# Expert stage of a two-layer model: weight splits traced a block earlier, gates and gathers respread, own buffers for the second half's first group

## The chip, the cores and the metric

The kernel runs on one core of a Trainium2 chip. The metric is the device time of one execution in microseconds; the median of three runs is given. The profile is of one further execution.

## The reference

The program is one large layer (a state-space branch, a dilated attention branch, a memory branch, and then a mixture of 16,384 tiny experts, "PEER") followed by two further layers (attention and a 32-expert mixture). All is float32, 512 tokens, model width 1024. The change lies in the PEER stage alone, which computes this:

```python
def _peer(hn, w_query, sub_keys, expert_down, expert_up):
    q = (hn @ w_query).reshape(b, s, PEER_HEADS, 2, PEER_QUERY_DIM // 2)      # 8 heads
    sc = einsum('bshcd,hckd->bshck', q, sub_keys)                             # 2 x 128 keys a head
    v1, i1 = top_k(sc[..., 0, :], 16);  v2, i2 = top_k(sc[..., 1, :], 16)
    cand = v1[..., :, None] + v2[..., None, :]                                # 256 a head
    top, pos = top_k(cand, 16)
    idx = i1 * 128 + i2 at pos;  gate = softmax(top)                          # 128 experts a token
    act = gelu(einsum('bld,blhkd->blhk', hb, expert_down[idx]))
    return einsum('blhk,blhkd->bld', gate * act, expert_up[idx])
```

## The kernel before

**Two ways to compute the experts.** The first 128 tokens (GAT) are done by gathering: for each of their 128 chosen experts a row of 1024 numbers is fetched for every token (an indirect DMA of 512 KB, issued by GpSimd, line 1045) and VectorE (DVE) reduces it against the token (line 1049, rows of expert_down) or adds it, weighted, to a sum (line 1058, rows of expert_up). That makes 2 x 128 steps, called rows here; the generator `gathered` gives one at each call, with five rows in buffers ahead. The other 384 tokens (DENSE) are done densely: all 16,384 experts are computed for them, and a matrix of gates that is zero but for the chosen ones weights the result.

**First half, `peer_down`, lines 1067 to 1135.** After the queries (16 products, lines 1090 to 1105) the dense part runs over 128 blocks of 128 experts. Each block loads a weight of 128x1024 (512 KB) into one of five `raw` buffers on SyncE's queue and splits it, by `wload` (line 250), into a rounded high part on ScalarE (ACT, line 267) and a low remainder on DVE (line 268). Each part has three buffers. TensorE (PE) then does 24 matmuls of 128x384 in three passes (lines 272 to 274) into one of four accumulators `acc`; ACT takes the gelu (line 1124) into one of two buffers `act`, and its own queue stores it to the DRAM tensor `actd` (line 1125).

**Routing beside it.** While the blocks run, DVE also works out the choice. `peer_select` is called for four chunks of 128 tokens (the first is for the gathered tokens; it sets `ready`, after which rows may run). `peer_gates` then builds the gate matrix of the three dense chunks: for each token two one-hot columns (`oa`, half of them on ACT, and `ob`, lines 1281 to 1288), one product of both on PE (line 1289), in 96 pieces of four tokens; a group of 32 tokens is stored to the DRAM tensor `gd` from GpSimd's queue (line 1292).

**What sets the order.** The blocks are a generator that gives way four times a block. Each such turn adds PACE to a credit, and the routing is advanced as long as credit is left; each of its steps names its cost in a `yield` (2.0, 0.8, 5.0, 2.3 in `peer_select`, 2.2 in `peer_gates`, while a selection that runs between the gates costs nothing). A second count, `due`, adds 0.27 a turn for the rows while routing lasts, and 0.5 after it. That is the order in which the instructions are listed. A planner in the kernel's framework (line 2113) then lays them out on the engines by its own timing: of what is ready on an engine, the earliest in the list goes first, so that the final order can differ from the list. On the chip each engine works through its own instructions in that final order.

**Second half, `peer_up`, lines 1137 to 1189.** Sixteen groups of eight blocks. For each group `weighted` loads the stored gelus and gates (`at`, `gt`, four blocks at a time, 768 KB each), multiplies them (every second one on GpSimd, POOL, line 1162) and splits the product into `c_hi` and `c_lo`: eight pieces a group. The pieces of the next group are listed between the eight tiles j of the present one. Each tile loads and splits a weight of expert_up, does 24 matmuls, adds the result to the residual `x` on DVE (line 1178), and advances the rows by 1.1. All of its buffers are in a pool "pu" opened after the first half's pools are closed, so the first group's loads, too, wait until those are free:

Of the kernel before, what the change touches and what calls it, by code (L numbers as in the profile page):

```python
# [24 lines left out]
KC = 8  # L25
# [12 lines left out]
RAW = 20  # L38
PACE = 0.68
GAT = 128  # L40
# [179 lines left out]
class Kernel:  # L220
# [55 lines left out]
    def proj_fm_g(self, src, act, kn=KC, engine=None):  # L276

        hi, lo = self.wload(src, kn * 128, engine)
        act = [[a[:, k] for k in range(kn)] if not isinstance(a, list) else a for a in act]
        n = act[0][0].shape[1]  # L280
        ps = self.ps("acc", [128, 512])
        for k in range(kn):
            sl = slice(k * 128, (k + 1) * 128)
            self.mm3(ps[:, :n], (hi[:, sl], lo[:, sl]), (act[0][k], act[1][k]), k == 0, k == kn - 1)
            if k == kn - 1:
                with self.tc.issue_after(self.last.ins):
                    next(self.side, None)
            if k % 2 == 1:
                yield
        return ps[:, :n]  # L290
# [731 lines left out]
    def peer(self):  # L1022

        TG = 32
        actd = self.dr.tile([128, 128, DENSE], F32, name="actd")
        gd = self.dr.tile([DENSE // TG, 128, 128 * TG], F32, name="gd")
        with self.pool("rows") as pr:
# [3 lines left out]
            self.peer_down(actd, gd, TG, st, rows)  # L1031
            self.peer_up(actd, gd, TG, rows)

# [32 lines left out]

    def peer_down(self, actd, gd, TG, st, rows):

        V, A, P, T, Q, I = self.V, self.A, self.P, self.T, self.Q, self.I
        with self.pool("u2") as up:  # L1070
            hn = [up.tile([128, KC, S], F32R, name=n) for n in ("hn_hi", "hn_lo")]
            acts = [up.tile([128, DENSE], F32, name=f"act{i}") for i in range(2)]
            st["hn"] = st["pool"].tile([128, D], F32, name="rhn", tag="rhn")
# [9 lines left out]
            with self.pool("pk", 1) as p1:  # L1083
                idxu = p1.tile([128, NT, 16, 16], U32, name="idxu")
                vals = p1.tile([128, NT, 16, 16], F32, name="vals")
                with self.pool("pk3", 2) as p2:
# [3 lines left out]
                    for hc in range(16):  # L1090
# [8 lines left out]
                        for c in range(NT):  # L1099
# [5 lines left out]
                            V.max_index(ix[:, 8:16], v[:, 8:16], sc[:, c])  # L1105

                with self.pool("pk2", 2) as p2:
                    def routing():
                        yield from self.peer_select(0, vals, idxu, p2, st)
                        sT = yield from self.peer_select(1, vals, idxu, p2)  # L1110
                        for c in range(1, NT):
                            nxt = _Work(self.peer_select(c + 1, vals, idxu, p2) if c + 1 < NT else iter(()))
                            for i, w in enumerate(self.peer_gates(c, sT, p2, gd, TG)):
                                yield w
                                if i % 4 == 0:
                                    yield next(nxt, 0.0)
# [4 lines left out]
                    def hidden():  # L1121
                        for i1 in range(128):
                            ps = yield from self.proj_fm_g(I["down"][i1], dense)
                            A.activation(acts[i1 % 2], ps, AF.Gelu)  # L1124
                            A.dma_start(actd[i1], acts[i1 % 2])
                    for i, _ in enumerate(hidden()):
                        credit += PACE
                        while credit > 0:
                            credit -= next(work, 1.0e9)
                        if st["ready"]:  # L1130
                            due += 0.27 if credit > -1e8 else 0.5
                            while due >= 1:
                                next(rows, None)
                                due -= 1
                    _run(work)

    def peer_up(self, actd, gd, TG, rows):
        V, A, P, T, Q, I = self.V, self.A, self.P, self.T, self.Q, self.I
        with self.pool("pu", 2) as p2:

            pair = lambda i: [p2.tile([128, 8, DENSE], F32R, name=f"c{i}_{n}", bufs=1) for n in ("hi", "lo")]
            odd = pair(1)
# [4 lines left out]
            def weighted(g):  # L1147

                hi, lo = parts[g % 2]
                for h in range(2):  # L1150
                    i0 = g * 8 + h * 4
                    at = p2.tile([128, 4, DENSE], F32, name="at")
                    queue = P if g == 0 else Q
                    queue.dma_start(at, actd[i0:i0 + 4].rearrange("i p t -> p i t"))
                    gt = p2.tile([128, DENSE // TG, 4, TG], F32, name="gt")
                    queue.dma_start(gt.rearrange("p j i t -> p j (i t)"),
                                gd.rearrange("j p x -> p j x")[:, :, i0 * TG:(i0 + 4) * TG])
                    for i in range(4):
                        k = h * 4 + i
                        a = at[:, i].rearrange("p (j t) -> p j t", t=TG)  # L1160
                        eng = P if i % 2 else V
                        eng.tensor_mul(a, a, gt[:, :, i])
                        self.split(hi[:, k], lo[:, k], at[:, i])
                        yield
                return hi, lo

            nxt, due = weighted(0), 0.0
            for g in range(16):
                hi, lo = _run(nxt)
                nxt = weighted(g + 1) if g < 15 else iter(())  # L1170
                for j in range(KC):
# [19 lines left out]
    def peer_select(self, c, vals, idxu, p2, st=None):  # L1191
# [17 lines left out]
        V.tensor_add(cand[:, :, starts[8]:], vv[:, :, 0, 8:16], vv[:, :, 1, 0:1].to_broadcast([128, 8, 8]))  # L1209
        yield 2.0  # L1210
        top = p2.tile([128, 8, 16], F32, name="top")
        posu = p2.tile([128, 8, 16], U32, name="posu")
        for h in range(8):
# [4 lines left out]
            V.max_index(posu[:, h, 8:16], top[:, h, 8:16], cand[:, h])  # L1218
            yield 0.8

# [21 lines left out]
        yield 5.0  # L1242
        sel = p2.tile([128, 3, 128], F32, name="sel")
        gate = gate.rearrange("p h k -> p (h k)")
        A.activation(sel[:, 2] if st is None else st["gate"], gate, AF.Copy)
        for n, ix in ((0, ia), (1, ib)):
            for z in range(2):
# [7 lines left out]
                V.tensor_reduce(sel[:, n, part], oh, axis=AX.X, op=ALU.add)  # L1255
            yield 2.3
        if st is not None:
# [11 lines left out]
    def peer_gates(self, c, sT, p2, gd, TG):  # L1269
# [3 lines left out]
        for j in range(128 // TG):  # L1273
            st = p2.tile([128, 128, TG], F32, name="gst")
            for t4 in range(TG // 4):
# [14 lines left out]
                A.activation(st[:, :, t4 * 4:t4 * 4 + 4], ps.rearrange("p t i -> p i t"), AF.Copy)  # L1290
                yield 2.2
            P.dma_start(gd[(c * 128 - GAT) // TG + j], st.rearrange("p i t -> p (i t)"))
# [825 lines left out]
```

## Time and profile before

| | us |
|---|---|
| median of three runs (lowest, highest) | 4564.19 (4563.07, 4568.98) |
| the profiled execution | 4570.65 |
| its span in the trace | 4568.8 |

The span's mean granted clock is 0.969 of full speed. Over the whole span PE is busy 4298.5 us (94%), DVE 2732.7 us (60%), ACT 1457.4 us (32%) and POOL 1227.5 us (27%). These shares are averages over many stages. The stage of the change lies at about 940 to 2206 us of the span: the first half up to about 1630, the second half after it. A busy share says nothing by itself; the stretches have to be compared one by one, and the waits named. In the wait and timeline views a number in brackets is the time for which the engine stood idle just before that instruction, with the instruction that released it. Durations on one engine overlap by some tens of nanoseconds, so that a sum of them is larger than the time in which the engine is busy.

### The profile page before, as it was taken

How to read it: one execution, taken by the hardware profiler on the slowest of the kernel's cores; microseconds unless marked ns; L12 is line 12 of the kernel's file. 1: busy time of each engine (PE TensorE's matmuls, PEld its weight loads, DVE VectorE, ACT ScalarE, POOL GpSimd, SP SyncE). 2: the span in 40 equal slices, each digit the busy share in tenths (PEclk: the TensorE clock that was granted, in tenths of full speed). 3: DMA queues.
4: the chain of work that ended last, by engine and by line, in shares of the span. 5: the costliest groups of instructions: out<-in, count | busy, mean ns of one | idle time of the engine just before them, and what ended most of it. 6: DMA issues, size and time to landing. Idle time of an engine off the chain costs nothing. (4 is left out here: it accounts for less than half of the span.)

```text
span 4568.8 us, 59963 instructions
## 1 busy us (share of the span) xinstructions
PE 4298.5 (94%) x21607; PEld 3271.1 (72%) x21607; DVE 2732.7 (60%) x5348; ACT 1457.4 (32%) x2579; POOL 1227.5 (27%) x883
## 2 busy tenths in 40 slices
PE   8998989998999869999999998999989999899997
PEld 7777777898999869999877774544448778545443
DVE  6577776799999789766458764222234665522122
ACT  5324443343677223333334331100122433200001
POOL 2153335017534554210113451000010345100000
PEclk9999999999999989999999998999999999899999
DMA  4133433348999999765334447988852122598986
GB/s 151 55 98 108 129 115 111 112 141 279 347 363 344 365 360 351 265 227 176 109 109 125 136 128 262 371 321 323 341 219 86 57 63 94 223 359 318 350 310 242
DMA packets 351617, 987.41 MB, mean 216 GB/s; under 512 B 34288, under 2 KB 114672, under 8 KB 349392
## 3 DMA queue, kind: packets, MB, share of 16 engines
q1 hardware_dynamic: 293488, 795.77, 49.0%
q0 software_dynamic: 39392, 162.55, 9.8%
q10 hardware_dynamic: 18432, 25.17, 1.5%
q8 instruction: 174, 2.85, 0.2%
q14 instruction: 131, 1.07, 0.1%
HBM read 926.70 MB, written 56.66 MB: 215 GB/s over the span
## 5 line engine op out<-in xcount | busy, mean ns | idle before, releaser
L267 ACT ACTIVATE whi<-raw 128x1024 fp32r<-128x1024 f32 (+3 forms) x582 | 568.2, 979 | 1196.7 <-PE acc L273 701.5
L268 DVE TENSOR_TENSOR wlo<-raw,whi 128x1024 fp32r<-128x1024 f32 (+4 forms) x438 | 536.3, 1227 | 247.6 <-ACT whi L267 227.8
L1752 PE MATMUL acc<-raw,xg 128*64 128x512 f32 (+1 forms) x2024 | 554.7, 599 | 0.0
L272 PE MATMUL acc<-hn_hi,whi 128*128 128x384 f32 (+1 forms) x1152 | 402.7, 350 | 26.8 <-ACT act L1124 26.5
L274 PE MATMUL acc<-hn_hi,wlo 128*128 128x384 f32 (+1 forms) x1152 | 401.0, 349 | 21.5 <-DVE wlo L268 21.5
L273 PE MATMUL acc<-hn_lo,whi 128*128 128x384 f32 (+1 forms) x1152 | 400.1, 347 | 0.0
L349 POOL TENSOR_TENSOR ssq<-ssq,sq 128x512 f32<-128x512 f32 (+1 forms) x22 | 31.4, 1440 | 1338.9 <-ACT sq L348 1338.8
L268 POOL TENSOR_TENSOR wlo<-raw,whi 128x1024 fp32r<-128x1024 f32 (+3 forms) x144 | 281.7, 1958 | 376.2 <-ACT whi L267 369.4
L272 PE MATMUL acc<-c_hi,whi 128*128 128x384 f32 x1024 | 342.7, 336 | 30.9 <-ACT c_hi L267 30.7
L1752 PEld LDWEIGHTS acc<-raw,xg 128*64 128x64 f32 (+1 forms) x2024 | 164.0, 140 | 283.6 <-issue 261.0
L274 PE MATMUL acc<-c_hi,wlo 128*128 128x384 f32 x1024 | 342.8, 336 | 5.1 <-DVE wlo L268 5.0
L273 PE MATMUL acc<-c_lo,whi 128*128 128x384 f32 x1024 | 343.1, 335 | 1.3 <-DVE c_lo L268 1.3
L1800 DVE SCALAR_TENSOR_TENSOR x<-t,mod,x 128x512 f32<-128x512 f32 x160 | 117.3, 749 | 250.0 <-PE t L1798 250.0
L463 DVE RECIPROCAL gate<-gate 128x512 f32<-128x512 f32 x72 | 241.0, 3347 | 36.1 <-POOL gate L462 36.0
L1774 PE MATMUL acc<-raw,h 128*64 128x512 f32 (+1 forms) x1000 | 253.2, 600 | 3.9 <-ACT h L1763 3.9
L272 PEld LDWEIGHTS acc<-hn_hi,whi 128*128 128x128 f32 x1152 | 218.9, 190 | 38.9 <-ACT act L1124 33.3
L274 PEld LDWEIGHTS acc<-hn_hi,wlo 128*128 128x128 f32 x1152 | 218.5, 190 | 31.6 <-DVE wlo L268 26.6
L273 PEld LDWEIGHTS acc<-hn_lo,whi 128*128 128x128 f32 x1152 | 218.8, 190 | 5.0 <-issue 0.2
L1045 POOL DMA_INDIRECT rows<-in_rows_up_dram,ridx x128 | 172.9, 1351 | 177.8 <-DVE racc L1058 150.4
L1045 POOL DMA_INDIRECT rows<-in_rows_down_dram,ridx x128 | 168.6, 1317 | 188.2 <-DVE ract L1049 95.8
L272 PEld LDWEIGHTS acc<-c_hi,whi 128*128 128x128 f32 x1024 | 193.0, 189 | 31.9 <-ACT c_hi L267 31.0
L272 PE MATMUL acc<-h_hi,whi 128*128 128x512 f32 x512 | 215.2, 420 | 0.4 <-ACT whi L267 0.4
(673 smaller groups left out, 9635.7 us busy)
## 6 DMA issues: line engine op xcount, KB each, us to landing
raw<-in_w_dram SPq DMA_DIRECT2D x756, 512.0 KB, 7.8
raw<-in_down_dram SPq DMA_DIRECT2D x128, 512.0 KB, 6.0
raw<-in_up_dram SPq DMA_DIRECT2D x128, 512.0 KB, 5.3
raw<-in_ada_dram SPq DMA_DIRECT2D x96, 512.0 KB, 3.9
raw<-in_w_gate_dram SPq DMA_DIRECT2D x72, 512.0 KB, 3.4
actd<-act ACTq DMA_DIRECT2D x128, 192.0 KB, 5.3
gd<-gst POOLq DMA_DIRECT2D x12, 2048.0 KB, 11.1
gt<-gd SPq DMA_DIRECT2D x30, 768.0 KB, 6.6
```

The source lines that it names most:

```text
L267: self.A.activation(hi, src, AF.Copy)
L268: (self.P if engine == "ap" else self.V).tensor_sub(lo, src, hi.bitcast(F32))
L272: T.matmul(out, lhsT=l[0], rhs=r[0], start=start, stop=False)
L273: T.matmul(out, lhsT=l[0], rhs=r[1], start=False, stop=False)
L274: self.last = T.matmul(out, lhsT=l[1], rhs=r[0], start=False, stop=stop)
L349: (eng or (self.V if k % 2 else self.P)).tensor_add(self.ssq[k % 2], self.ssq[k % 2], sq)
L463: V.reciprocal(d, d)
L1045: P.indirect_dma_start(r, None, self.I[n], bass.IndirectOffsetOnAxis(ap=st["idx"][:, kk:kk + 1], axis=0))
L1752: T.matmul(ps[i * m:(i + 1) * m], lhsT=xg[:, kk, o + i * m:o + (i + 1) * m], rhs=w[i][:, k * 512:(k + 1) * 512], start=kk == 0, stop=kk == 7)
L1774: T.matmul(po[h][i * m:(i + 1) * m], lhsT=hh[:, f, i * m:(i + 1) * m], rhs=w[i][:, h * 512:(h + 1) * 512], start=f == 0, stop=f == 3)
L1800: V.scalar_tensor_tensor(self.x[:, k], ps, mod[:, 40 + k:41 + k], self.x[:, k], op0=ALU.mult, op1=ALU.add)
```

## The change

- `hidden` holds the next block's weight: `wload` of block i+1 is listed before block i's matmuls. `proj_fm_g` takes an already split weight.
- There are three gelu buffers instead of two.
- PACE is 0.5 instead of 0.68. In `peer_select` the costs are 2.4, 1.2 a head, 1.8 after every second of the seven arithmetic steps (instead of 5.0 after all of them) and 4.6; in `peer_gates` 1.2 instead of 2.2. A step of the next selection is listed after every second piece of gates, not every fourth.
- Rows advance by 0.25 a turn while routing lasts, 0.35 after it, and 1.05 a tile in the second half.
- When the routing has been listed, the loop over the blocks is left; a pool "first" is opened with `c_hi`, `c_lo` and one buffer each of `at` and `gt`; the blocks go on, and a piece of the first group is listed at every fourth turn, its loads on GpSimd's queue. The group's high and low parts serve the even groups afterwards.
- In the second half the rest of a group's pieces is listed at the end of its last tile; a one-element memset is gone.

```diff
-PACE = 0.68
+PACE = 0.5
-        hi, lo = self.wload(src, kn * 128, engine)
+        hi, lo = src if isinstance(src, tuple) else self.wload(src, kn * 128, engine)
...
+            def begin():
+                pf = stack.enter_context(self.pool("first", 1, side="right"))
+                st["first"] = self.group(pf, 0, 1)
+            self.peer_down(actd, gd, TG, st, rows, begin)
+            self.peer_up(actd, gd, TG, rows, st["first"])
+    def group(self, pool, i, bufs):
+        return [pool.tile([128, 8, DENSE], F32R, name=f"c{i}_{n}", bufs=1) for n in ("hi", "lo")] + [(pool, bufs)]
+    def weighted(self, g, actd, gd, TG, tiles, queue):
+        hi, lo, (pool, bufs) = tiles
+        for h in range(2):
+            i0 = g * 8 + h * 4
+            at = pool.tile([128, 4, DENSE], F32, name="at", bufs=bufs)
+            queue.dma_start(at, actd[i0:i0 + 4].rearrange("i p t -> p i t"))
+            gt = pool.tile([128, DENSE // TG, 4, TG], F32, name="gt", bufs=bufs)
+            queue.dma_start(gt.rearrange("p j i t -> p j (i t)"),
+                            gd.rearrange("j p x -> p j x")[:, :, i0 * TG:(i0 + 4) * TG])
+            for i in range(4):
...
+                eng = self.P if i % 2 else self.V
+                eng.tensor_mul(a, a, gt[:, :, i])
+                self.split(hi[:, k], lo[:, k], at[:, i])
+                yield
...
-            acts = [up.tile([128, DENSE], F32, name=f"act{i}") for i in range(2)]
+            acts = [up.tile([128, DENSE], F32, name=f"act{i}") for i in range(3)]
...
+                def hidden():
+                    nxt = self.wload(I["down"][0])
+                    for i1 in range(128):
+                        w, nxt = nxt, self.wload(I["down"][i1 + 1]) if i1 < 127 else None
+                        ps = yield from self.proj_fm_g(w, dense)
+                        A.activation(acts[i1 % 3], ps, AF.Gelu)
+                        A.dma_start(actd[i1], acts[i1 % 3])
+                hid = hidden()
...
-                                if i % 4 == 0:
+                                if i % 2 == 0:
                                     yield next(nxt, 0.0)
...
-                    for i, _ in enumerate(hidden()):
+                    for _ in hid:
                         credit += PACE
                         while credit > 0:
                             credit -= next(work, 1.0e9)
+                        if credit < -1e8:
+                            break
                         if st["ready"]:
-                            due += 0.27 if credit > -1e8 else 0.5
+                            due += 0.25
...
+            begin()
+            first = self.weighted(0, actd, gd, TG, st["first"], P)
+            for i, _ in enumerate(hid):
+                due += 0.35
+                while due >= 1:
+                    next(rows, None)
+                    due -= 1
+                if i % 4 == 0:
+                    next(first, None)
+            _run(first)
...
-            nu = p2.tile([128, 512], F32, name="nu", tag="nu", bufs=3)
-            V.memset(nu[:, 0:1], 0.0)
-            parts = [pair(0), odd]
+            other = self.group(p2, 1, 2)
+            parts = [first[:2] + other[2:], other]
...
-                    due += 1.1
+                    due += 1.05
...
-                    if g == 14 and j == KC - 1:
-                        _run(rows)
+                    if j == KC - 1:
+                        _run(nxt)
+                        if g == 14:
+                            _run(rows)
```

The five cost edits in `peer_select` and `peer_gates` are listed above.

## Rows read from the trace of the kernel before

**Rows 1.** Stretch, its length, busy us (instructions) by engine, clock, DMA share, GB/s

```profile
940.00:1200.00 260.00, 238.01 (x1380) 232.44 (x1379) 253.03 (x763) 123.06 (x221) 135.52 (x111) 0.98 0.74 256
1200.00:1350.00 150.00, 149.71 (x963) 148.90 (x962) 148.38 (x351) 104.82 (x240) 64.25 (x56) 1.00 0.94 351
1350.00:1473.00 123.00, 117.47 (x765) 115.03 (x764) 120.41 (x332) 94.48 (x233) 46.04 (x42) 0.99 0.93 349
1473.00:1637.50 164.50, 133.52 (x743) 127.77 (x742) 122.79 (x100) 47.02 (x65) 95.79 (x68) 0.99 0.98 364
...
1700.00:1875.00 175.00, 169.69 (x967) 166.97 (x966) 162.34 (x192) 63.73 (x88) 78.68 (x60) 1.00 0.97 344
1875.00:2206.00 331.00, 331.00 (x1917) 330.97 (x1916) 206.48 (x263) 116.60 (x151) 47.32 (x34) 1.00 0.59 195
```

**Rows 2.** Waits of PE, 940 to 2206 us: total us, times, longest

```profile
PE acc L274 <- DVE wlo L268: 26.5, 21, 5.8
PE acc L272 <- ACT act L1124: 26.5, 20, 1.6
PE s L1289 <- DVE ob L1288: 1.6, 2, 1.0
```

**Rows 3.** Line 272 by stretch: PE and weight loads, clock, DMA

```profile
1200.00:1350.00 150.00, 76.95 (x222) 41.88 (x222) 1.00 0.94 351
```

**Rows 4.** Line 1289 by stretch, same columns

```profile
1200.00:1350.00 150.00, 45.84 (x293) 43.80 (x291) 1.00 0.94 351
```

**Rows 5.** Groups on DVE, 944 to 1640 us: busy us, mean ns, idle before

```profile
L268 DVE TENSOR_TENSOR wlo<-raw,whi 128x1024 fp32r<-128x1024 f32 x128 | 159.2, 1245 | 40.2 <-ACT whi L267 27.2 <-DMA raw<-in_up_dram 8.2 <-DMA raw<-in_down_dram 4.8
L1049 DVE CUSTOM_DVE_ANT_0 rows<-rows,rhn 128x1024 f32<-128x1024 f32 x128 | 158.4, 1248 | 4.2 <-DMA rows<-in_rows_down_dram,ridx 4.2
L1288 DVE TENSOR_SCALAR ob<-const,sT 128x128 f32<-128x128 f32 x384 | 128.2, 371 | 0.0
```

**Rows 6.** Timeline around a wait for a split: start, duration in us

```profile
1129.54 1.22 DVE L1049 CUSTOM_DVE_ANT_0 rows<-rows,rhn 128x1024 f32<-128x1024 f32 x1
...
1132.98 2.35 DVE L268 TENSOR_TENSOR wlo<-raw,whi 128x1024 fp32r<-128x1024 f32 x2
...
1134.25 0.54 PE L274 MATMUL acc<-hn_hi,wlo 128*128 128x384 f32 x1 [4.28 <-DVE wlo L268]
```

**Rows 7.** Timeline of ACT in the first half's tail

```profile
1528.18 1.06 ACT L267 ACTIVATE whi<-raw 128x1024 fp32r<-128x1024 f32 x1 [3.10 <-PE acc L273]
1529.14 0.47 ACT L1124 ACTIVATE act<-acc 128x384 f32<-128x384 f32 x1
...
1530.02 0.49 ACT L1124 ACTIVATE act<-acc 128x384 f32<-128x384 f32 x1 [0.40 <-ACT act L1124]
```

**Rows 8.** Timeline at the change of halves

```profile
1649.50 0.82 POOL L1154 DMA_DIRECT2D at<-actd  x1 [1.11 <-issue]
...
1658.90 1.03 DVE L1162 TENSOR_TENSOR at<-at,gt 128x384 f32<-128x384 f32 x2 [4.66 <-DMA gt<-gd]
...
1660.12 1.33 PE L272 MATMUL acc<-c_hi,whi 128*128 128x384 f32 x3 [30.69 <-ACT c_hi L267]
```

**Rows 9.** Line 1058 (rows of expert_up) by stretch: DVE, clock, DMA

```profile
1473.00:1637.50 164.50, 86.71 (x68) 0.99 0.98 364
...
1700.00:1875.00 175.00, 53.85 (x41) 1.00 0.97 344
```

**Rows 10.** Groups on DVE, 1663 to 2206 us

```profile
L268 DVE TENSOR_TENSOR wlo<-raw,whi 128x1024 fp32r<-128x1024 f32 x126 | 170.2, 1351 | 18.1 <-ACT whi L267 17.9
...
L1058 DVE SCALAR_TENSOR_TENSOR racc<-rows,ract,racc 128x1024 f32<-128x1024 f32 x50 | 66.8, 1336 | 0.1
...
L1162 DVE TENSOR_TENSOR at<-at,gt 128x384 f32<-128x384 f32 x62 | 51.4, 869 | 10.9 <-DMA at<-actd 9.2 <-issue 1.6
```

**Rows 11.** Groups on POOL, the same stretch

```profile
L1162 POOL TENSOR_TENSOR at<-at,gt 128x384 f32<-128x384 f32 x62 | 81.3, 1333 | 222.0 <-DMA at<-actd 211.4 <-DVE wlo L268 8.8 <-DMA gt<-gd 1.5
```

**Rows 12.** DMA issues of the whole run: KB each, us to landing

```profile
actd<-act ACTq DMA_DIRECT2D x128, 192.0 KB, 5.3
```

More of the change, by code (lines that the diff above doesn't have):

```diff
@@ L1026, in peer @@
         gd = self.dr.tile([DENSE // TG, 128, 128 * TG], F32, name="gd")
-        with self.pool("rows") as pr:
+        with self.pool("rows") as pr, contextlib.ExitStack() as stack:
             st = {"pool": pr, "idx": pr.tile([128, 128], U32, name="ridx"), "gate": pr.tile([128, 128], F32, name="rgate"),
@@ L1030, in peer @@
             rows = self.gathered(st)
-            self.peer_down(actd, gd, TG, st, rows)
-            self.peer_up(actd, gd, TG, rows)
+            def begin():
[15 more added lines that the diff above has]
+            for i in range(4):
+                k = h * 4 + i
+                a = at[:, i].rearrange("p (j t) -> p j t", t=TG)
+                eng = self.P if i % 2 else self.V
+                eng.tensor_mul(a, a, gt[:, :, i])
+                self.split(hi[:, k], lo[:, k], at[:, i])
+                yield
+        return hi, lo
     def gathered(self, st):
@@ L1065, in gathered, with peer_down @@
             V.tensor_add(x, x, tr)
-    def peer_down(self, actd, gd, TG, st, rows):
+    def peer_down(self, actd, gd, TG, st, rows, begin):
         V, A, P, T, Q, I = self.V, self.A, self.P, self.T, self.Q, self.I
@@ L1120, in peer_down @@
                     work, credit, due = routing(), 0.0, 0.0
[L1121 to L1125, printed above, removed]
-                    for i, _ in enumerate(hidden()):
+                    for _ in hid:
                         credit += PACE
@@ L1135, in peer_down, with peer_up @@
                     _run(work)
-    def peer_up(self, actd, gd, TG, rows):
+            begin()
[8 more added lines that the diff above has]
+            _run(first)
+    def peer_up(self, actd, gd, TG, rows, first):
         V, A, P, T, Q, I = self.V, self.A, self.P, self.T, self.Q, self.I
         with self.pool("pu", 2) as p2:
-            pair = lambda i: [p2.tile([128, 8, DENSE], F32R, name=f"c{i}_{n}", bufs=1) for n in ("hi", "lo")]
-            odd = pair(1)
-            nu = p2.tile([128, 512], F32, name="nu", tag="nu", bufs=3)
-            V.memset(nu[:, 0:1], 0.0)
-            parts = [pair(0), odd]
[L1147 to L1167, printed above, removed]
+            other = self.group(p2, 1, 2)
+            parts = [first[:2] + other[2:], other]
+            due = 0.0
             for g in range(16):
-                hi, lo = _run(nxt)
-                nxt = weighted(g + 1) if g < 15 else iter(())
+                hi, lo = parts[g % 2][:2]
+                nxt = self.weighted(g + 1, actd, gd, TG, parts[(g + 1) % 2], Q) if g < 15 else iter(())
                 for j in range(KC):
@@ L1209, in peer_select @@
         V.tensor_add(cand[:, :, starts[8]:], vv[:, :, 0, 8:16], vv[:, :, 1, 0:1].to_broadcast([128, 8, 8]))
-        yield 2.0
+        yield 2.4
         top = p2.tile([128, 8, 16], F32, name="top")
@@ L1218, in peer_select @@
             V.max_index(posu[:, h, 8:16], top[:, h, 8:16], cand[:, h])
-            yield 0.8
+            yield 1.2
         gate = p2.tile([128, 8, 16], F32, name="gate")
@@ L1241, in peer_select @@
             V.tensor_sub(ib, ib, tmp)
-        yield 5.0
+            if a % 2:
+                yield 1.8
         sel = p2.tile([128, 3, 128], F32, name="sel")
@@ L1255, in peer_select @@
                 V.tensor_reduce(sel[:, n, part], oh, axis=AX.X, op=ALU.add)
-            yield 2.3
+            yield 4.6
         if st is not None:
@@ L1290, in peer_gates @@
                 A.activation(st[:, :, t4 * 4:t4 * 4 + 4], ps.rearrange("p t i -> p i t"), AF.Copy)
-                yield 2.2
+                yield 1.2
             P.dma_start(gd[(c * 128 - GAT) // TG + j], st.rearrange("p i t -> p (i t)"))
```

## The prediction

> **What bounds the kernel now.** I read the 40 slices of the page first: TensorE is busy in nine tenths of nearly every slice, so only stretches with gaps can give anything, and the change touches the expert stage alone, about 940 to 2206 us. Then the busy time by stretch [rows 1], where the reader is to compare, line by line, what PE and DVE lack of the stretch's length. Then who PE waited for [rows 2], and last the timeline around three kinds of wait [rows 6 to 8].
>
> The clean rate comes from the end of the second half, 1875 to 2206 us, where PE has no gap: 331 us for 1917 matmuls, 0.1727 us each, so 24 of them (one expert block, or one tile j of the second half) take 4.144 us [rows 1]. A one-hot matmul of the gates costs (149.71 - 222 x 3 x 0.1727) / 293 = 0.118 us [rows 1, 3, 4]. The first half has 128 blocks and 384 one-hot products (one for each ob [rows 5]), which the trace holds as two matmuls each, 768: 530 + 91 = 621 us of PE work. It runs from 940 to 1660.1 - 30.7 = 1629.4 us [rows 8], so 689 us: 68 us are lost there. DVE is busy 253.0 + 148.4 + 120.4 + 122.8 = 645 us over the first four stretches [rows 1], more than PE needs. So DVE bounds the first half, PE the second, where DVE does 206 of the last 331 us. PE's waits name the places: 30.7 us once, at the change of halves, for the first split of the second half [rows 8]; 26.5 us in 20 waits for the gelu (ACT act); 26.5 us in 21 waits for the weights' low part (DVE wlo) [rows 2].
>
> **The change part by part.** Every gain or loss is against the profiled execution, 4570.65 us. That is 6.46 us above the median of the runs (4564.19), and I take 6.46 off at the end.
>
> *The first group in buffers of its own.* Before, the second half's pool lies where the first half's activations lay, so its four loads leave at 1649.5 us and later, after the last block; the first multiply starts at 1658.90 and PE at 1660.1 [rows 8]. Now these loads (two of actd, two of gd, 768 KB each) are issued from POOL's queue about 42 blocks before the end, and eight pieces follow, one a block. What moves: 4 multiplies and 8 subtractions on DVE (about 0.55 to 0.87 us each, 8 us), 4 multiplies on POOL (1.333 us, 5.3 us) [rows 10, 11], 8 copies on ACT, 3.1 MB or some 9 us at 364 GB/s [rows 1]. The second pair of loads waits for the first pair's four pieces, since there is one buffer of each, and the gathers queued behind it on POOL wait too; five are ahead in buffers, so I count nothing. The cover is DVE's spare time in the last 42 blocks: by the list they hold 1.4 gathered rows a block, 1.24 + 1.4 x 1.34 = 3.1 of 4.144 us, 44 us to spare [rows 5, 10]. Without the cover, 8 + 5 us come back. What is late next is the first up-weight, split ahead in three buffers as every block. Gain 29 of 30.7, less the first tile's own start; ends 25 and 31.
>
> *A third gelu buffer.* Between 1473 and 1637.5 PE waits for a gelu that ACT runs after the split of a later block, and two gelus follow one another (1529.14 and 1530.02): ACT is up to four blocks behind, the number of accumulators [rows 7]. With two buffers each gelu needs the store of two blocks before, which takes 5.3 us to land [rows 12]. A third gives 12.4 instead of 8.3 us. The list also falls from 2 to 1.4 gathered rows a block there, so less memory traffic beside it: DMA is at 0.98 and 364 GB/s in this stretch [rows 1], 0.52 + 0.20 + 2 x 0.52 = 1.76 MB a block, and then 1.45 MB, or 350 GB/s at PE's rate. Gain 20 of 26.5; if the order on ACT and not the buffer makes the wait, 6; at best 25.
>
> *Weights split a block ahead, routing and gathers respread.* The moved split brings its 512 KB load on SP's queue, 1.06 us on ACT and 1.24 us on DVE with it; ACT waits for PE to free a weight buffer already, so the lead is set by three buffers and the edit only lifts the split above row work of the same block. The trace shows what that is worth at 1129.5 to 1134.25: row reductions of 1.22 us go first, then two splits, and PE waits 4.28 us [rows 6]. The list itself, worked out from the costs in the code: before, 2.72 credits a block put the routing into 386 turns or 96.5 blocks, with 97 rows, and 63 more after it, 160 in the first half. After, 2.0 credits a block and dearer selections (28.4 for 18) with cheaper gates (1.2 for 2.2) make 344 turns or 86 blocks, 72 rows, then 42 blocks with 59 rows: 131. The last four of a selection's twelve steps used to run in one burst at the end of a chunk of gates; its now fifteen steps all fit between the gates. The trace has 197 rows at 1637.5 (128 down, one first up, 68 up [rows 9]). With 66 fewer, DVE's first half falls by 66 x 1.27 = 84 us (1.27 lies between the 1.248 and 1.336 of rows here and in the second half [rows 5, 10]), to 561 plus 8 of the first group: 569 of PE's 621. So PE bounds it. Idle PE in 940 to 1200 is 22.0 us [rows 1]; I take 12 back. The bounds: 20, if only single waits are left, and -5, if the gate products (on DVE now behind the lifted splits) hold PE instead. The respread credits cost no instruction of their own.
>
> *More rows in the second half.* By the list 125 rows are left for it, at 1.05 a tile, which lasts 119 of the 120 tiles before the last group; the trace has 59 after 1637.5. The nearest row has just this density: 1700 to 1875 us, 41 rows [rows 9] over 967 / 24 = 40.3 tiles, 4.35 us a tile, DVE busy 4.03 us a tile and DMA at 0.97 [rows 1]. So each of the some 66 further tiles costs 4.35 - 4.144 = 0.21 us: 14 us lost. Bounds: 4 lost if rows still run ahead into the first half; 30 if a tile costs twice as much over its clean time. The last rows now end some 33 us before the end instead of 330, still before their transposes are wanted.
>
> Row: a DVE multiply of the second half takes 0.869 us on average where the same-sized POOL one takes 1.333, and the split of a weight 1.351 us against 1.245 in the first half [rows 5, 10, 11]: DVE is held up there while POOL multiplies. The Trainium skill (SBUF — State Buffer, Who interferes with whom) has the two engines share one pair of ports under an exclusive lock, so that the later one stands still for the whole instruction. By that rule the lock, not the sum of DVE's own work, fills a tile, which is the second rival; the lengthened rows agree with the rule in kind, and bear out about a tenth of a microsecond of it for a split.
>
> **Sum.** 29 + 20 + 12 - 14 = 47 us. 4570.65 - 47 = 4523.7, less 6.46: 4517 us.
>
> **The rivals.** (1) *Order follows readiness, not the list.* The instructions are put in order by a planner, and 197 rows against 160 listed say that it runs rows ahead when DVE has a hole. Then the first half stays full: 29 + 14 + 0 - 6 = 37 us gained, 4527. Against it: between 1700 and 1875 rows keep close to the list (1.02 a tile for 1.1).
> (2) *The second half becomes DVE-bound.* Each tile has half a POOL multiply, 0.67 us. If half of that stops DVE beyond what the lengthened durations hold, DVE needs 4.03 + 0.33 us, over PE's time, and with the idle share of that stretch a tile takes some 4.6 us: 30 us more over 119 tiles, 4547. Against it: the stretch of equal density took 4.35.
> (3) *The gelu wait stays*, since it comes from ACT's order: 4 of 20, gain 31, 4533. For it: the split stands first on ACT in [rows 7]; against: the store's landing is longer than a block.
> (4) *Slower: the one-hot matmuls take the wait.* With the splits lifted, what DVE does last is the gates' one-hot columns. They stand in PE's one queue in 96 pieces of 8, each fed by four ob (0.371 us [rows 5]) and two oa. In the first two chunks the list gives DVE a selection and 32 pieces in 19.2 blocks. If PE then waits at each piece for half its columns, 0.75 us, that is 72 us: 25 slower, 4589. It decides from 47 / 96 = 0.49 us a piece. For it: DVE is 98% busy in 940 to 1473 [rows 1]; against: PE waited for a column only 1.6 us in all [rows 2].
> (5) *All terms at their good end*, 31 + 25 + 20 - 4 = 72 and some of the first half's other losses: 4485.
>
> **How the numbers follow.** Forecast 0.43 (4500 to 4532); rival 1 0.17; rival 2 0.13; rival 3 0.10; rival 4 0.10; rival 5 0.07. About 0.2% (9 us) is what a measurement of this kernel can tell from no change. Faster by more than that: all but rival 4 and the worse ends of 2 and 3, 0.80. Within: 0.08, from those ends. Slower: 0.12, rival 4 and an unlucky second rival. The range reaches from rival 5 with a few microseconds of the unnamed losses, 4478, to the worst sum of the bounds (25 + 6 - 5 - 30 = -4, about 4568): 4478 to 4566.
>
> **What would show it.** In the changed profile: the wait of PE at the change of halves under 5 us; waits for act under 7 us in all; rows done at that point near 131 (about 190 would be rival 1); DVE's share of the first half down to about 91%, PE without 4 us gaps there; rows running until shortly before the last group, and tiles of 4.3 to 4.4 us up to there. Tiles over 4.5 us are rival 2, waits of L1289's matmuls for ob or oa rival 4. The prediction is wrong if the second half or the gate stretch gives back over 30 us, or if the stages after 2206 us move.

## The result and the profile after

| | before | after |
|---|---|---|
| median of five runs each, side by side (lowest, highest), us | 4563.07 (4558.73, 4568.98) | 4518.01 (4510.25, 4531.27) |
| ratio after / before (95% interval) | | 0.9904 (0.9884 to 0.9924) |
| profiled execution, its span, us | 4570.65, 4568.8 | 4515.67, 4513.8 |
| last gelu of the first half starts | 1637.5 | 1598.0 |
| first matmul of the second half | 1660.1 | 1586.6 |
| last x add of the second half | 2205.5 | 2158.7 |

45 us faster, 1 us from the forecast. Within the stage, the first half ends 39.5 us earlier. The change of halves gives 34.0 us: a gap of 22.6 us between the last gelu and the next matmul has become an overlap of 11.4. The second half takes 572.1 us instead of 545.4 and so gives 26.7 back. The sum is 46.8 us, at the stage's end. The two profiled executions lie 55 us apart; the other 8 us arise in later layers that the change does not touch. There the time from the first to the last instruction of one line (398) is between 1190 and 1198 us in all the kernels of this study, in no order with their parts, so I take it for scatter.

The stretches after (columns as in [rows 1]):

```profile
940.00:1200.00 260.00, 243.16 (x1414) 235.85 (x1413) 253.13 (x756) 128.25 (x234) 131.10 (x108) 0.99 0.74 255
1200.00:1350.00 150.00, 150.00 (x959) 150.00 (x958) 145.09 (x336) 98.46 (x222) 71.22 (x57) 1.00 0.95 355
1350.00:1440.00 90.00, 90.00 (x572) 89.97 (x570) 76.42 (x174) 55.82 (x121) 34.58 (x29) 1.00 0.93 346
1440.00:1586.50 146.50, 143.81 (x900) 143.16 (x899) 121.26 (x234) 85.57 (x183) 53.60 (x50) 1.00 0.95 354
1586.50:1700.00 113.50, 100.49 (x526) 97.89 (x525) 100.73 (x112) 36.17 (x52) 48.61 (x42) 0.91 0.99 344
1700.00:1875.00 175.00, 168.24 (x942) 166.12 (x941) 158.33 (x177) 58.59 (x79) 82.10 (x62) 0.98 0.94 324
```

The tail of the first half, where PE was busy 133.5 of 164.5 us [rows 1], is now nearly full. DVE, 98% busy from 1350 to 1473 before, is at 83 to 85% from 1350 on. The holes have moved to 1586 to 1875, the start of the second half. The waits of PE there and in the first half, 940 to 2170 (answers [rows 2]: total us, times, longest):

```profile
PE acc L274 <- DVE wlo L268: 24.6, 21, 4.6
PE acc L272 <- ACT c_hi L267: 5.2, 1, 5.2
PE acc L272 <- DVE c_lo L268: 3.6, 2, 1.8
PE acc L272 <- ACT act L1141: 2.7, 2, 1.3
```

The waits for the gelu are gone (26.5 to 2.7), the waits for the weights' low part are not (26.5 to 24.6). At the change of halves the first tile waits 0.2 us instead of 30.7 [rows 8]; one group later there is a wait of 5.2. That group's buffers lie in the old pool, and its loads stand on SyncE's queue behind five weight loads, each of which waited until a split on DVE had freed a raw buffer (22.8 us in all, 1586.5 to 1612). The last of the five left at 1608.05, the group's first load right behind it:

```profile
1591.35 17.03 SPq L252 DMA_DIRECT2D raw<-in_up_dram  x5
1608.48 0.38 SPq L1049 DMA_DIRECT2D at<-actd  x1
...
1626.88 1.33 PE L272 MATMUL acc<-c_hi,whi 128*128 128x384 f32 x3 [5.24 <-ACT c_hi L267]
```

That wait is not the largest item. In the second half's first 240 us, 1586.5 to 1826.6, PE waits 19.7 us in all, and nearly half of it for the low part of the up-weights, which DVE makes:

```profile
PE acc L274 <- DVE wlo L268: 9.4, 5, 3.1
PE acc L272 <- ACT c_hi L267: 5.2, 1, 5.2
PE acc L272 <- DVE c_lo L268: 3.6, 2, 1.8
```

ACT in the tail (answers [rows 7]): in this piece each gelu stands right behind one split, and its store right behind the gelu. Before, two splits could pass without a gelu, and then two gelus came together.

```profile
1524.21 1.06 ACT L267 ACTIVATE whi<-raw 128x1024 fp32r<-128x1024 f32 x1 [2.36 <-PE acc L273]
...
1525.77 0.49 ACT L1141 ACTIVATE act<-acc 128x384 f32<-128x384 f32 x1
1526.29 0.33 ACTq L1142 DMA_DIRECT2D actd<-act  x1
1529.27 1.06 ACT L267 ACTIVATE whi<-raw 128x1024 fp32r<-128x1024 f32 x1 [3.01 <-PE acc L273]
1530.24 0.47 ACT L1141 ACTIVATE act<-acc 128x384 f32<-128x384 f32 x1
```

Rows of expert_up by stretch (answers [rows 9]; DVE busy us (count), clock, DMA, GB/s). With one first row and 128 rows of expert_down before, 154 rows are done at the change of halves and 158 at the last gelu (there 197 before). They end at 2021.6 (before 1874):

```profile
1440.00:1586.50 146.50, 31.97 (x25) 1.00 0.95 354
1586.50:1700.00 113.50, 37.08 (x29) 0.91 0.99 344
1700.00:1875.00 175.00, 48.58 (x38) 0.98 0.94 324
1875.00:2100.00 225.00, 46.77 (x35) 1.00 0.82 284
```

DVE's groups in the second half (answers [rows 10]) and the stores of the gelus over the whole run (answers [rows 12]: median us to landing). A store takes no less time than before:

```profile
L268 DVE TENSOR_TENSOR wlo<-raw,whi 128x1024 fp32r<-128x1024 f32 x127 | 169.4, 1343 | 12.7 <-ACT whi L267 12.7
L1086 DVE SCALAR_TENSOR_TENSOR racc<-rows,ract,racc 128x1024 f32<-128x1024 f32 x101 | 131.2, 1299 | 0.4
...
L1057 DVE TENSOR_TENSOR at<-at,gt 128x384 f32<-128x384 f32 x60 | 59.6, 1034 | 3.0 <-issue 2.2 <-DMA gt<-gd 0.8
```

```profile
actd<-act ACTq DMA_DIRECT2D x128, 192.0 KB, 5.5
```

### The profile page after: what moved, and what is told of

Read it like the earlier page. It is cut to its first block, busy times and chain, and to the rows that moved or that the text cites. A ratio compares the mean times of both kernels' runs of the same rounds, so it can differ in the third digit from the quotient of the medians.

```text
span 4513.8 us, 60036 instructions
## 1 busy us (share of the span) xinstructions
PE 4287.2 (95%) x21607; PEld 3269.0 (72%) x21607; DVE 2741.7 (61%) x5347; ACT 1454.2 (32%) x2579; POOL 1226.3 (27%) x883
```

## Experiments

Medians are in us; each ratio is to the kernel before, run on the same chip beside it (median 4562.5 to 4565.1). In the diffs + is what the experiment has, and ... stands for lines left out.

**1. The third gelu buffer.** The kernel before with that buffer alone:

```diff
-            acts = [up.tile([128, DENSE], F32, name=f"act{i}") for i in range(2)]
+            acts = [up.tile([128, DENSE], F32, name=f"act{i}") for i in range(3)]
...
```

> The kernel before with a third gelu buffer and nothing else. Theory A (each term of the sum is a wait of its own and goes by its own edit): PE's waits for the gelu fall from 26.5 us to under 7, time 20 us below before (bounds 6 to 25). Rival (the wait comes from ACT's order, in which a later block's split stands first, not from the number of buffers): waits for the gelu stay above 20 us, time within 6 us of before. The wait at the change of halves stays at 30 us by both.

4530.34, ratio 0.9931 (0.9915 to 0.9948). One buffer is worth 32 us. The last gelu comes 41.5 us earlier (1596.0), more than the whole change reached (39.5). The wait at the change of halves stays:

```profile
PE acc L272 <- ACT c_hi L267: 26.2, 1, 26.2
PE acc L274 <- DVE wlo L268: 24.6, 16, 5.8
PE acc L272 <- ACT act L1124: 2.7, 2, 1.3
```

The reverse, the changed kernel with two buffers again:

```diff
-            acts = [up.tile([128, DENSE], F32, name=f"act{i}") for i in range(3)]
+            acts = [up.tile([128, DENSE], F32, name=f"act{i}") for i in range(2)]
...
```

> The changed kernel with two gelu buffers again. Theory B (after the single parts: the third buffer is nearly the whole first-half gain, whatever the pacing): the wait for the gelu is back at 20 to 30 us, the first half ends 30 to 45 us later, time 30 us or more above the changed kernel. Rival (fewer rows in the first half free ACT and DMA too, so that two buffers would do with the new pacing): time within 15 us of the changed kernel, gelu waits under 10 us.

4563.4, ratio 1.0000 (0.9991 to 1.0010): all of the gain is gone. The waits for the gelu are back:

```profile
PE acc L272 <- ACT act L1141: 30.3, 18, 11.6
```

Is it the store that takes too long behind ACT's next split? The kernel before with the stores issued from SyncE:

```diff
-                            A.dma_start(actd[i1], acts[i1 % 2])
+                            Q.dma_start(actd[i1], acts[i1 % 2])
```

> The kernel before with its two gelu buffers, but the stores of the gelus are issued on SyncE's queue, not behind the splits on ACT's. Theory that a store stuck behind ACT's next split (which waits for PE) is what makes two buffers too few: waits for act fall from 26 to under 8 us, the first half's last gelu comes some 35 to 40 us earlier, the kernel takes 4528 to 4535. Rival, that the landing itself (5.3 us median, up to 12) against two blocks of 4.1 us is enough for the wait: over 18 us of act waits stay, 4555 to 4565. If stores now stand behind weight loads that wait for a buffer, the waits grow and it is slower than before.

4564.87, ratio 0.9999 (0.9990 to 1.0008): no. Freed from ACT's queue, the stores change nothing:

```profile
PE acc L272 <- ACT act L1124: 25.3, 20, 1.7
```

ACT's timeline in that kernel shows why. The order has stayed: three splits, the second followed by one gelu, the third by two.

```profile
1520.40 1.06 ACT L267 ACTIVATE whi<-raw 128x1024 fp32r<-128x1024 f32 x1 [3.55 <-PE acc L273]
1524.56 1.06 ACT L267 ACTIVATE whi<-raw 128x1024 fp32r<-128x1024 f32 x1 [3.10 <-PE acc L273]
1525.52 0.47 ACT L1124 ACTIVATE act<-acc 128x384 f32<-128x384 f32 x1
1530.35 1.06 ACT L267 ACTIVATE whi<-raw 128x1024 fp32r<-128x1024 f32 x1 [4.36 <-PE acc L273]
1531.31 0.85 ACT L1124 ACTIVATE act<-acc 128x384 f32<-128x384 f32 x2
```

So I counted, along ACT's timeline of each kernel, which later block's split each gelu stands behind (a gelu of block i behind the split of block i+3, i+5, ...):

| gelus of blocks 96 to 127, ahead of them the split of | i+3 | i+4 | i+5 | i+6 | waits for act |
|---|---|---|---|---|---|
| before | 1 | 1 | 14 | 16 | 26.5 |
| two buffers, store from SyncE | 1 | 1 | 13 | 17 | 25.3 |
| after with two buffers | 0 | 0 | 16 | 16 | 30.3 |
| before with three buffers | 8 | 2 | 20 | 2 | 2.7 |
| after | 20 | 4 | 5 | 3 | 2.7 |

The waits go with i+6. The split of block i+6 can start only when PE has finished with the weights of block i+3 (three buffers of each part: ACT waits for PE's line 273). PE's block i+4 wants block i's accumulator (there are four), so it waits for that split and for the gelu: 1.06 + 0.47 us. The longest waits of line 272 for act are 1.3 to 1.7 us, but for one of 11.6. The order on ACT is fixed in the program, and the number of gelu buffers decides it. The landing of the store on the chip does not: it takes as long in the kernels without the wait. That the planner puts the gelu late because its own timing makes it wait for a buffer is the plausible link; it was not tried by itself.

**2. The first group's own buffers.** Those alone: the changed kernel with three things put back.

```diff
-            acts = [up.tile([128, DENSE], F32, name=f"act{i}") for i in range(3)]
+            acts = [up.tile([128, DENSE], F32, name=f"act{i}") for i in range(2)]
...
-                        w, nxt = nxt, self.wload(I["down"][i1 + 1]) if i1 < 127 else None
-                        ps = yield from self.proj_fm_g(w, dense)
+                        ps = yield from self.proj_fm_g(I["down"][i1], dense)
...
-PACE = 0.5
+PACE = 0.68
...
```

> Only the first group's own buffers; two gelu buffers, the weight split at the block's start, and all old pacing numbers. Theory A: the 30.7 us wait at the change of halves goes, time 24 to 29 us below before, gelu waits stay near 26 us. Rival (the loads land in the stretch where DMA is full, 364 GB/s, and push the weights back): the wait goes but 10 us or more come back in the stretch before it, time 15 us below before or less.

4562.98, ratio 0.9994 (0.9984 to 1.0004): nothing. The gap at the change is gone (first matmul at 1632.8, 15.3 us ahead of the last gelu, so 38 us gained there). But the first half ends 10.6 us later, and the second takes 571.7 instead of 545.4 us. The second half's first 240 us show the place. Before, after, this kernel (columns as above):

```profile
1660.10:1780.10 120.00, 114.50 (x636) 112.23 (x637) 115.23 (x136) 44.97 (x65) 59.64 (x48) 0.97 1.04 367
1780.10:1900.10 120.00, 118.88 (x686) 117.89 (x685) 104.82 (x123) 40.43 (x52) 46.81 (x34) 1.00 0.89 311
```

```profile
1586.60:1706.60 120.00, 106.99 (x563) 104.39 (x562) 105.13 (x116) 38.63 (x55) 52.17 (x45) 0.91 0.98 343
1706.60:1826.60 120.00, 113.24 (x627) 111.12 (x626) 108.75 (x126) 41.08 (x58) 52.49 (x40) 0.97 0.94 321
1826.60:1986.60 160.00, 159.79 (x913) 159.24 (x912) 148.51 (x166) 53.16 (x70) 80.25 (x58) 1.00 0.96 337
```

```profile
1632.80:1752.80 120.00, 105.25 (x556) 101.81 (x555) 103.25 (x113) 35.90 (x50) 59.79 (x45) 0.93 1.02 355
1752.80:1872.80 120.00, 115.16 (x636) 113.38 (x635) 107.30 (x124) 41.96 (x59) 51.10 (x40) 0.97 0.92 318
```

At 0.1727 us a matmul, the 240 us lose 240 - 0.1727 x 1322 = 11.7 us before, 34.5 after and 34.1 here. The rows in them are about as many (50, 56, 56), although this kernel has the old paces and 191 rows done when its second half starts: the loss does not come from rows moved into the second half. In the changed kernel's next 160 us 38 rows run with DMA at 0.96, and PE loses some 2 us.

Would the second group in buffers of its own help? Both groups are listed to be loaded and split within the first half:

```diff
+                st["second"] = self.group(pf, 1, 1)
...
-            first = self.weighted(0, actd, gd, TG, st["first"], P)
+            first = itertools.chain(self.weighted(0, actd, gd, TG, st["first"], P), self.weighted(1, actd, gd, TG, st["second"], P))
```

> The changed kernel with buffers outside the first half's memory for the second group as well, loaded and split before the first half ends; the pieces listed beside group 0's tiles fall away. Theory G (the wait at the change of halves moved to group 1, 5.2 us, and the slow clock after it costs as much again): that wait goes and the second half is 8 to 14 us shorter. Rival D (transfers and VectorE work put off come back): the same time within 4 us, the waits turn up before the change of halves or later.

4520.9, ratio 0.9893 (0.9876 to 0.9910): as after. The second group's loads share one buffer with the first's and stand among the gathers on POOL's queue. The last left at 1617.6, 20 us after the last gelu, so the second group still came late, and the many small waits turn into one:

```profile
PE acc L272 <- ACT c_hi L267: 20.8, 1, 20.8
```

The 120 us with this wait hold 534 matmuls, the next 120 us 681, against 563 and 627: what was behind seems to catch up while PE stands, as it may have done before the change in its 30.7 us. The loss of the 240 us is 30.2 us, about the same. What a second group that really comes early would give, no run shows.

**3. The split a block ahead, and the pacing.** First the changed kernel without the split ahead, then with all the old paces (PACE, the costs in `yield`, the rows' advance):

```diff
-                    nxt = self.wload(I["down"][0])
...
-                        ps = yield from self.proj_fm_g(w, dense)
+                        ps = yield from self.proj_fm_g(I["down"][i1], dense)
```

> The changed kernel with each weight split listed at its own block's start again. Theory A (the earlier listing lifts the splits above row work): PE's waits for the low part in the first half grow by 5 to 12 us and so does the time. Rival (three weight buffers set the lead, the place in the list nothing): the same time within 3 us and the same waits.

```diff
-PACE = 0.5
+PACE = 0.68
...
-                            due += 0.25
+                            due += 0.27
...
-                due += 0.35
+                due += 0.5
...
-                    due += 1.05
+                    due += 1.1
...
```

> The changed kernel with all old pacing numbers (credits, costs, rows a turn and a tile). Theory A (12 us won in the first half by fewer rows there, 14 us lost in the second by more): the same time within 5 us; rows done at the change of halves near 195 instead of 155; the first half some 12 us longer, the second some 14 us shorter. Rival (DVE bounded the first half, and spreading is what freed it): 15 us or more slower than the changed kernel.

4511.94 (ratio 0.9890, 0.9872 to 0.9909) and 4522.09 (0.9920, 0.9900 to 0.9940). Neither differs from the change's 0.9904 beyond the intervals: each of these two parts, taken out alone, is worth nothing that can be measured. Both at once, beside three buffers, were not taken out. With the old paces 163 rows are done at the change of halves, not the 195 expected.

**4. What costs the second half's start.** The changed kernel with the weighted row sums on DVE cut to 8 of 1024 columns, the gathers as they are (this leaves out the gathered tokens' result):

```diff
-                    V.scalar_tensor_tensor(acc, r, act[:, k:k + 1], acc, op0=ALU.mult, op1=ALU.add)
+                    V.scalar_tensor_tensor(acc[:, :8], r[:, :8], act[:, k:k + 1], acc[:, :8], op0=ALU.mult, op1=ALU.add)
```

> The changed kernel with the weighted sum over gathered rows of expert_up cut to 8 of 1024 columns: all gathers stay, VectorE is freed of 127 times 1.28 us; the gathered tokens' result is left out. Theory S or L (VectorE holds the second half back): second half near PE's own 540 us, 25 us shorter or more. Rival D (the gathers' traffic holds it back): within 8 us of the changed kernel.

The opposite, sums whole but no gathers of expert_up:

```diff
+                if n == "rows_down":
...
+                else:
+                    r = last
```

> The changed kernel without the gathers of the 128 rows of expert_up (64 MB of traffic and 128 issues on GpSimd); DVE's 128 weighted sums stay as they are, on a row that is already there, so the gathered tokens' output is left out. Theory that memory traffic (DMA at 0.94 to 0.99 in the first 290 us of the second half) costs the second half its 40 us over PE's bare time: the half takes 554 us as when the sums were cut, the kernel 4500. Theory that DVE and the lock with POOL's multiplies cost it: the half stays at 572 within 6, the kernel at 4518 within 6, and the waits for wlo stay over 15 us. If the two share it, 563 and 4510.

4503.54 (0.9861, 0.9845 to 0.9878) and 4480.77 (0.9817, 0.9804 to 0.9831). With the sums cut the second half takes 553.8 us instead of 572.1, between the two theories. Without the gathers it takes 541.9, more gained than any of the theories had, and the first half ends 10 us earlier. From 1590 to 1875 DVE is full, and yet PE loses only 285 - 0.1727 x 1613 = 6 us (the changed kernel, with 1450 matmuls there, 35):

```profile
1590.00:1700.00 110.00, 108.51 (x613) 106.55 (x612) 109.97 (x130) 42.08 (x58) 28.42 (x17) 1.00 0.80 256
1700.00:1875.00 175.00, 174.94 (x1000) 174.08 (x999) 174.88 (x201) 61.33 (x82) 36.84 (x24) 1.00 0.69 221
```

So a full DVE is not by itself the bound: with the gathers gone, the start of the half runs at nearly PE's rate. The second group's first load then leaves 0.4 us after the last gelu's start (1587.7) and not 10.5, and no wait for `c_hi` is left, though its buffers lie in the old pool as before:

```profile
1588.13 0.38 SPq L1049 DMA_DIRECT2D at<-actd  x1
```

Nor are the gathers alone the bound, since cutting DVE's sums beside all of them gave 18 us. Whether they act by their bytes (DMA 0.98 against 0.80) or by GpSimd's work in issuing them stays open, since both went.

The changed kernel with all gate multiplies on DVE, none on POOL:

```diff
-                eng = self.P if i % 2 else self.V
-                eng.tensor_mul(a, a, gt[:, :, i])
+                self.V.tensor_mul(a, a, gt[:, :, i])
```

> The changed kernel with all of the second half's gate multiplies on VectorE, none on GpSimd. Theory L (splits of 1.22 us that take 3 to 4.6 us in the second half stand still while GpSimd multiplies): the longest splits fall to about 1.3 us, the second half gets 8 to 15 us shorter although VectorE does 60 more multiplies of 0.55 us (33 us). Rival S (VectorE's sum of work bounds it): 33 us more work make the second half 10 us longer or more. Rival D (transfers bound it): no change within 4 us.

4502.27 (0.9860, 0.9844 to 0.9877), every run below every run of the changed kernel: the best whole kernel here, 16 us ahead of the change. DVE does twice the multiplies in the same time (second half, as above):

```profile
L268 DVE TENSOR_TENSOR wlo<-raw,whi 128x1024 fp32r<-128x1024 f32 x129 | 156.7, 1219 | 10.7 <-ACT whi L267 10.7
...
L1056 DVE TENSOR_TENSOR at<-at,gt 128x384 f32<-128x384 f32 x120 | 58.7, 550 | 5.0 <-DMA gt<-gd 2.2 <-issue 1.5 <-DMA at<-actd 1.3
```

The same edit on the kernel before with three gelu buffers:

```diff
-            acts = [up.tile([128, DENSE], F32, name=f"act{i}") for i in range(2)]
+            acts = [up.tile([128, DENSE], F32, name=f"act{i}") for i in range(3)]
...
-                        eng = P if i % 2 else V
-                        eng.tensor_mul(a, a, gt[:, :, i])
+                        V.tensor_mul(a, a, gt[:, :, i])
```

> The kernel before with two edits: the third gelu buffer, and all gate multiplies on DVE, none on POOL. Theory that POOL's multiplies hold DVE up wherever they run: the 16 us that this edit gave the changed kernel come on top of the 32 of the buffer, 4514 or a little less, and the second half falls from 550 to about 535 us. Rival, that the hold-up costs time only where rows fill DVE (the changed second half has 102 rows, this one some 60): the second half moves by under 6 us, 4524 to 4532.

And on the changed kernel without the split ahead:

```diff
-                eng.tensor_mul(a, a, gt[:, :, i])
+                self.V.tensor_mul(a, a, gt[:, :, i])
...
-                        ps = yield from self.proj_fm_g(w, dense)
+                        ps = yield from self.proj_fm_g(I["down"][i1], dense)
```

> The changed kernel with all gate multiplies on DVE and without the split a block ahead. If the two are independent and the split ahead is worth nothing: 4496 to 4504 (the first gave 4502, the second took 6 off the changed kernel, inside its interval). If the split ahead pays once DVE is no longer held up, this is slower than 4506.

4526.05 (0.9913, 0.9898 to 0.9927) and 4506.06 (0.9869, 0.9855 to 0.9884). On the old structure the edit gives 4 us, inside the intervals, and not 16. Its second half is 8 us shorter (542.0 against 549.8), but PE waits at the change of halves as before (26.9). The split ahead gives nothing here either. The losses of the first 240 us, all worked out as above:

| kernel | loss, us | second half, us |
|---|---|---|
| before | 11.7 | 545.4 |
| before, three gelu buffers | 16.0 | 549.8 |
| the same, multiplies on DVE | 7.4 | 542.0 |
| first group's buffers alone | 34.1 | 571.7 |
| after | 34.5 | 572.1 |
| after, second group's buffers too | 30.2 | 573.2 |
| after, multiplies on DVE | 18.1 | 556.4 |
| after, row sums cut | 18.4 | 553.8 |
| after, no gathers | 6.3 | 541.9 |

## Why the prediction was right, and where its steps were not

The time was met, 4518 for 4517. The sum was too, 47 forecast and 46.8 us at the stage's end. The terms were not: their errors cancelled, and that is luck.

- *First half, 20 + 12 forecast, 39.5 measured.* The step that failed is the cause of the gelu waits. I let the third buffer work through the landing of the store, 12.4 for 8.3 us, and held ACT's order for a rival that would keep the wait. It is ACT's order, and the buffer sets that order (1). The size was off with it. I stopped at 20 of the 26.5 us that the waits of line 272 showed; but when the gelus leave the splits' way, the tail's block falls from 5.3 us (164.5 us for 743 matmuls, 36 us more than at PE's rate) to nearly PE's rate, and 41.5 us go with the buffer alone. Rival 3 fell: the wait went.
- *Split ahead and respread, 12.* Nothing that can be measured, each alone (3). The 12 us of holes that I meant to fill in 940 to 1200 did go down by 5 (PE busy 243.2 for 238.0), yet waits for wlo of 15.0 us remain in the first half (21.5 before, and 14.4 without the split ahead), one of them 4.6 us long. And 39 rows left the first half, not 66. DVE had less to do, but in a shorter half: its share is 92% to the change of halves (595.9 of 646.5 us), and was 92% before (644.6 of 697.5), so that sign showed nothing.
- *The list.* My sum for it was wrong. A selection's steps carry their costs between the gates as well; the text on the kernel before says that they cost nothing, and I counted them before the change (386 turns) but not after it. With them the routing takes 457 turns after the change, 114 blocks and not 86, and 119 rows stand in the first half, not 131. The trace agrees: the last one-hot product is at 1525.0 and the first group's first load at 1538.2, some 14 blocks before the last gelu and not 42. So the cover for the first group was a third of what I took.
- *First group, 29.* At the place it gave 34, and the wait at the change went as forecast. The step that failed is the cover: what is late next. I named the first up-weight alone. PE then waits for the low parts of several up-weights (9.4 us), for the second group (5.2), whose first load leaves at 1608.48, and for low parts of later pieces (3.6); with the lower clock, 22.8 us more are lost in 240 us than before (34.5 - 11.7). Alone the edit is worth nothing (2). Beside the buffer the kernel goes from 4530.34 to 4518.01; these two intervals overlap, but the changed kernel without the split ahead, 4511.94 (0.9872 to 0.9909), is clear of the buffer alone (0.9915 to 0.9948).
- *More rows, -14; the second half gave back 26.7.* The size fell within its bounds (4 to 30), but the reason was wrong: with 191 rows done at its start the second half gave back as much (2). I took 0.21 us a tile from 1700 to 1875 of before; that stretch was itself in the start of the half. Where the further rows really run, 1826.6 to 1986.6, a tile takes 160 x 24 / 913 = 4.21 us, and 39 such tiles lose some 2.5 us. The 4.3 to 4.4 that I named as a sign were seen nowhere: 240 x 24 / 1190 = 4.84 us first, then 4.21.
- *Rival 1* had the mechanism: the planner ran 39 rows ahead of the list (158 for 119) as it had before (197 for 160), but without the price. *Rival 2* was right in part. Its sign, tiles over 4.5 us, was seen in the first 240 us, and moving POOL's multiplies to DVE gave 16 us in this kernel; but DVE's work alone does not bound the half (full without loss when the gathers are gone). Whether that is DVE's shorter instructions alone, or also gathers that no longer stand behind multiplies on POOL's queue, was not separated. The Trainium skill (SBUF — State Buffer, Who interferes with whom) says that a DVE instruction with two inputs in SBUF contends with GpSimd's reads; the runs agree: 1.034 us a multiply beside POOL's, 0.550 without. I had weighed the rule by the split alone, 0.1 us. *Rival 4*: waits for ob 0.8 us in the gate stretch, so nothing. *Rival 5* did not come.

## What to carry to other kernels

Before sizing an output buffer by how long its store takes, look at the order on the engine that fills it: where a consumer stands behind a later block's producer, one more buffer can change the order and be worth most of a stage's gain. A wait removed at a stage's start is gained only as far as the next pieces keep up: here 34 us were won at the place and 23 lost in the 240 us behind it, and the standstill had probably been the time in which DVE and the transfers caught up (a reading that fits the runs, not one that a run shows by itself). And test the parts of a change alone: here one more buffer carried 32 of 45 us, the first group's buffers gave nothing without it, and the rest nothing that could be measured.

## What the runs showed of the hardware

Two engines on one stream of multiplies gained DVE nothing: 60 multiplies of 128x384 beside POOL's other 60 kept DVE busy 59.6 us, all 120 alone 58.7 us; the split of a weight fell from 1343 to 1219 ns as well. Why 16 us of kernel time go with it was not separated from what the gathers on POOL's queue gain.

A wait of PE costs more than its own length. After the 20.8 us wait of the kernel in which the second group has buffers too, matmuls follow at 0.32 us (each row 0.32 after the last) until 1654.3, where full stretches run at 0.173. The granted clock from 1648 to 1652 is 0.50, the lower of TensorE's two levels, 1.2 instead of 2.4 GHz:

```profile
1648.39 1.33 PE L272 MATMUL acc<-c_hi,whi 128*128 128x384 f32 x3 [20.79 <-ACT c_hi L267]
1649.52 0.52 PE L273 MATMUL acc<-c_lo,whi 128*128 128x384 f32 x1
1649.84 0.52 PE L274 MATMUL acc<-c_hi,wlo 128*128 128x384 f32 x1
```

In the changed kernel, 1586.5 to 1875 has a granted clock of 0.91 and then 0.98. PE is busy there for 268.7 us on 1468 matmuls that take 253.5 at the full rate: 15 us of the loss go with the lower clock, 20 with waiting.
